# A network's first conditioning made feature tile by feature tile, with the first two hidden tiles multiplied behind each of them

## The chip, the cores and the metric

The kernel runs on one core of a Trainium2 chip. The metric is the device time of one execution in microseconds (us), lower is better. TensorE (PE in the profile, with its weight loads on a row of their own, PEld), VectorE (DVE), ScalarE (ACT) and GpSimd (POOL) work beside each other; the transfers that matter here are issued on SyncE's queue (SP), which takes them strictly in order.

## What is computed

The reference runs one transformer block and then two more blocks of another kind over 256 tokens of width 1024 (and a context of 256 tokens). Only the first lines of the first block touch the change:

```
mod = silu(c) @ w_ada + b_ada                 # (1, 9*1024)
sh1, sc1, gt1, ... = split(mod, 9)
y = rmsnorm(h, norm_ffn1) * (1 + sc1) + sh1   # 256 tokens x 1024 features
h = h + 0.5 * gt1 * swiglu(y, w_ffn1_gu, w_ffn1_down)
# swiglu: (silu(y @ w_gate) * (y @ w_up)) @ w_down, hidden width 2816 = 22 tiles of 128
```

The first conditioning is the pair sh1 and sc1: two vectors of 1024 values, each a product of silu(c) with a 1024 x 1024 piece of w_ada, 4 MB of f32 apiece. The first network cannot begin its matrix products before a feature tile of y (128 features x 256 tokens) has its scale and its shift.

## The kernel before

Activations lie feature-major: feature tile d of 8, 128 features on the partitions, tokens along the free dimension. Each f32 operand of a large product is split into a rounded high part and a remainder (H and L: `cut` and `split`, a cast on ACT, L149, and a subtraction on DVE, L150), and `mm3` (L172 to L174) issues three products H*H, H*L and L*H. For a hidden tile f of the network, `up` makes a gate and an up product, each over 8 feature tiles, 48 products of 256 columns in all; then silu, multiply and split give the hidden tile. 22 hidden tiles are followed by 8 output tiles (`down`) of 66 products each.

The start of the kernel (L664 to L706) does this, in program order:

1. Scale. The 4 MB of scale weights come in 8 loads `raw` (L672, 512 KB each, rows of a feature tile k). Each is the moving operand of products with the one column silu(c) as weights (L674), which gather the whole scale as two rows of 512 in two PSUM banks. f32 operands make every product two passes, so there are 32 passes of 512 columns. All 8 loads must be in before the scale is whole. The two rows are copied out and turned into columns by 8 products of one column (L689, 16 passes), and `settle` adds the bias and the gain.
2. The norm of x. Among the loads x arrives (1 MB, L676), and `row_of` broadcasts c over 128 partitions (L223). Squares on ACT, sums on DVE, `finish` (L329 to L343) leaves the reciprocal norm of each token, broadcast, in a PSUM bank.
3. u = x * scale * norm for 8 tiles (L693), then per tile the shift: `unit` loads 512 KB of transposed shift weights and sums their product with the broadcast silu(c) along the rows on DVE (L270). L701 (ACT) writes yH with the shift as bias, L702 (DVE) writes yL.
4. Three tiles of gate and up weights are loaded and cut in between (`ready`), and the context (1 MB, L704) is loaded behind the last shift tile; all later weight loads are queued behind that shift tile too (`first_loads`).

Hidden tiles f = 0 and f = 1 hold a bank each for gate and up (`mm`, `sc`, two buffers of each), so all four banks are open for them; from f = 2 on gate and up share one bank. Buffers: 8 slots for `raw`, 4 for the weight loads `wraw`, 3 each for their H and L.

The order of the instructions on each engine, and which load gets which slot, is fixed at build time by a planner that goes by program order as priority, by its own estimate of what is ready and by free slots. Later conditioning (`pump`) is put 400 places behind. Inside one PSUM bank the planner keeps writes of TensorE and reads of other engines in program order.

Of the kernel before, what the change touches and what calls it, by code (L numbers as in the profile page):

```python
# [10 lines left out]
F32 = mybir.dt.float32  # L11
BF16 = mybir.dt.bfloat16
F32R = mybir.dt.float32r
I32 = mybir.dt.int32
AF = mybir.ActivationFunctionType
OP = mybir.AluOpType
AX = mybir.AxisListType.X

P = 128
# [54 lines left out]
def trace(tc, A, dbg=None):  # L74
# [12 lines left out]
    def tl(pl, shape, dt, tag, bufs=None):  # L87
        kw = {} if bufs is None else {"bufs": bufs}
        return pl.tile(shape, dt, name=tag, tag=tag, **kw)

    def f32(ap):
        return ap.bitcast(F32)
# [11 lines left out]
    def bank(tag, shape=None):  # L104
        return tl(psum, shape or [P, 512], F32, tag)
# [70 lines left out]
    def split(H, L, x, copy=None):  # L176
        (copy or act.copy)(H, x)
        vec.tensor_tensor(L, x, f32(H), op=OP.subtract)  # L178
# [226 lines left out]
    def norm_of(seg, finish=True):  # L405
        n = Norm(seg)
        for d in range(ND):
            n.add(d)
        if finish:
            n.finish()  # L410
        return n


    def resid_add(ps, d, segs, keys, ch, norms):
        for s in segs:
# [4 lines left out]
            if norms is not None:  # L420
                norms[s].add(d)

    def up(w_gu, f, sub, hH, hL, tags):

        feed = Feed(w_gu, 2 * f)
        gH, gL = feed.next()
        uH, uL = feed.next()
        n = T * len(sub)
        ys = slice(sub[0] * T, sub[0] * T + n)
        if n == 512 or w_gu == "w1_gu" and f < 2:  # L430
            pg = bank("mm", [P, n])
            pu = bank("sc", [P, n])
        else:
            pb = bank(tags[f % 2])
            pg = pb[:, :T]
            pu = pb[:, T:]
        for ps, H, L in ((pg, gH, gL), (pu, uH, uL)):
            for k in range(ND):
                w = slice(k * P, k * P + P)
                mm3(ps, H[:, w], L[:, w], yH[:, k, ys], yL[:, k, ys], k == 0, k == ND - 1)  # L440
        sg = tl(tpool, [P, 512], F32, "sg", 2)
        act.activation(sg[:, :n], pg, AF.Silu)
        h = tl(tpool, [P, 512], F32, "hf", 2)
        vec.tensor_tensor(h[:, :n], sg[:, :n], pu, op=OP.mult)
        split(hH, hL, h[:, :n])

    def ahead(pools, w_gu, seg, out):

# [3 lines left out]
            up(w_gu, f, [seg], *out[f], ("mm", "mm"))  # L452
            yield

    def ffn_steps(hp, nslot, w_gu, w_dn, keys, gate_ch, segs, norms, lead=0, done=None, pre=None):

        N = T * len(segs)  # L460
        both = len(segs) == 2
        tags = ("mm", "sc")
        pre = pre or {}
        hs = {}

        def hidden(f):
            t = [tl(hp, [P, N], F32R, x, nslot) for x in ("hH", "hL")]
            hs[f] = {q: [x[:, i * T:i * T + T] for x in t] for i, q in enumerate(segs)}
            hs[f]["all"] = t
            if f in pre:  # L470
                hs[f][segs[1]] = pre[f]

        def ups(f, sub):
            up(w_gu, f, sub, *hs[f]["all" if len(sub) == len(segs) else sub[0]], tags)

        def down(ps, feed, k0, k1, part):
            whole = len(part) == len(segs) and not any(k in pre for k in range(k0, k1))
            W = [feed.block() for _ in range(k0, k1)]
            for i, q in enumerate(["all"] if whole else part):
                o = ps if whole else ps[:, i * T:i * T + T]  # L480
                for k in range(k0, k1):
                    mm3(o, *W[k - k0], *hs[k][q], k == k0, k == k1 - 1)

        groups = GROUPS if both or w_dn in GROUPED else ((0, NF),)
        for gi, (k0, k1) in enumerate(groups):
            last = gi == len(groups) - 1
            fs = list(range(k0, k1))
            if gi == 0 and lead:
                for f in fs[:lead]:
                    hidden(f)  # L490
                for i, q in enumerate(segs):
                    if i:
                        flush()
                    for f in fs[:lead]:
                        ups(f, [q])
                        tick(-(-ND // lead))
                        yield
                fs = fs[lead:]
            for f in fs:
                hidden(f)  # L500
                ups(f, segs[:1] if f in pre else segs)
                yield
            for q in segs:
                need(keys[q], gate_ch)
            for part in ([[q] for q in segs] if last else [segs]):
                feed = Feed(w_dn, k0)
                for d in range(ND):
                    ps = bank(tags[d % 2], [P, T * len(part)])
                    down(ps, feed, k0, k1, part)
                    resid_add(ps, d, part, keys, gate_ch, norms if last else None)  # L510
                    tick(1)
                    yield
                if last and done is not None:
                    flush()
                    for q in part:
                        done(q)

    def ffn(w_gu, w_dn, keys, gate_ch, segs, to, norms, done=None, lead=0, start=0.0, by=1.0, hook=None, pre=None,
            nslot=0):
        both = len(segs) == 2  # L520
        with ExitStack() as st:
            hp = pool("ffn_h", stack=st)
            steps = ffn_steps(hp, nslot or (12 if both or w_dn in GROUPED else 22), w_gu, w_dn, keys, gate_ch, segs, norms, lead, done, pre)
            n = NF + ND * (len(GROUPS) if both or w_dn in GROUPED else 1) + (lead + ND if both else 0)
            first = upos[0]
            for i in range(n):
                pump_to(first + (to - first) * min(1.0, max(0.0, (i + 1) / n - start) / (by - start)))
                next(steps)
                if hook is not None:
                    hook(i)  # L530
            for _ in steps:
                pass
# [129 lines left out]
    with ExitStack() as st:  # L662

        tp0 = pool("start", stack=st)  # L664
        csil = tl(tp0, [P, ND], F32, "csil")
        nc.sync.dma_start(csil, A["c_fm"])
        act.activation(csil, csil, AF.Silu)
        scp = [bank("sc", [1, 512]) for _ in range(2)]
        late = list(range(ND))
        for k in range(ND):  # L670
            raw = tl(tp0, [P, D], F32, "raw", 8)
            nc.sync.dma_start(raw, A["wada_sc"][k])  # L672
            for j in range(2):
                pe.matmul(scp[j], csil[:, k:k + 1], raw[:, j * 512:j * 512 + 512], start=k == 0, stop=k == ND - 1)  # L674
            if k == 1:
                nc.sync.dma_start(r[:, :, :T], A["xT"])  # L676
                row_of("c")
                nm = norm_of(0, False)
            if k == 4:
                nm.finish()  # L680
            if k in (3, 5):
                unit("wada", 0, late[0], s1, tl(tp0, [P, D], F32, "raw", 8))
                late.pop(0)
        pt = bank("tp", [P, ND])
        for j in range(2):
            row = tl(tpool, [P, 512], F32, "sg", 2)[:1, :]
            act.copy(row, scp[j])
            for d in range(4):
                pe.matmul(pt[:, 4 * j + d:4 * j + d + 1], row[:, d * P:d * P + P], one1, start=True, stop=True)  # L689
        settle("1", 1, pt)  # L690
        u = tl(tp0, [P, ND, T], F32, "u")
        for d in range(ND):
            vec.scalar_tensor_tensor(u[:, d, :], r[:, d, :T], modA["1"][:, d:d + 1], nm.rb, op0=OP.mult, op1=OP.mult)  # L693
        for d in range(ND):
            if d in late:
                dma = unit("wada", 0, d, s1, tl(tp0, [P, D], F32, "raw", 8))
                if d in (4, 5, 6):
                    ready["w1_gu", d - 4] = cut(load(A["w1_gu"][d - 4]))
            sh = mod["1"][:, d:d + 1]
            vec.tensor_tensor(sh, sh, V("b_ada", d), op=OP.add)  # L700
            act.activation(yH[:, d, :T], u[:, d, :], AF.Identity, bias=sh)  # L701
            vec.scalar_tensor_tensor(yL[:, d, :T], u[:, d, :], sh, f32(yH[:, d, :T]), op0=OP.add, op1=OP.subtract)  # L702
        first_loads[0] = dma
        queued(nc.sync.dma_start(r[:, :, T:], A["ctxT"]), dma)  # L704
        last_load[0] = dma
# [12 lines left out]
        if i >= NF - 1:  # L718
            run(nC[0], 1)

    ffn("w1_gu", "w1_dn", ["1"], 2, [0], upto["c0", 1], nm, next_norm(nm, ["1"], 1), hook=hook, by=FBY)
    run(fill, 2)
    tick(4)
    run(fill, 0)
# [720 lines left out]
def prepare(i):  # L1445
# [18 lines left out]
    for n in ("c", "c_2", "c_ctx_2"):  # L1464
        a[n] = i[n].reshape(-1)
    a["wada"] = _wt(i["w_ada"][0])
    a["wada_sc"] = i["w_ada"][0][:, D:2 * D].reshape(ND, P, D)
    a["c_fm"] = _fm(i["c"])
    a["wmod0"], a["wmod1"] = _wt(i["w_mod_2"][0]), _wt(i["w_mod_2"][1])
    for n, g, d in (("w1", "w_ffn1_gu", "w_ffn1_down"), ("w2", "w_ffn2_gu", "w_ffn2_down")):  # L1470
# [44 lines left out]
```

## Time and profile before

| | us |
|---|---|
| three runs, median (lowest to highest) | 2415.01 (2412.6 to 2419.7) |
| profiled execution, its own time | 2415.01 |
| span of the profiled execution, first to last instruction | 2413.3 |
| time outside the span | 1.7 |

The profile is of one execution. Times in it are from the start of the span. A matmul row on PE lasts longer than the distance to the next one, since products are pipelined: what a product costs in a stream is the distance between starts. The granted clock of TensorE has two levels here, 1.2 and 2.4 GHz (0.50 and 1.00 in the column PEclk); the column says 1.00 before the first recorded change, which lies at about 27 us.

### The profile page before, as it was taken

Reading aid. Unit: us, or ns where it says so; the run is one execution under the profiler, and the core shown is the slowest. Engines: PE = TensorE matmul, PEld = TensorE weight load, DVE = VectorE, ACT = ScalarE, POOL = GpSimd, SP = SyncE. Lnnn points to the kernel's source line nnn. Section 1 sums busy time; section 2 is a strip of 40 time slices with the busy share of each in tenths; the row PEclk is TensorE's granted clock in tenths of the full one; section 3 lists DMA queues with packets and bytes.
Section 4 is the critical chain, followed back from the end, with each engine's and each line's share of the span. In section 5 each row is a group of like instructions: output and inputs, shape, how many; then the busy total and the mean of one; then the engine's idle time right before and its main releaser. Section 6 shows DMA issues by size and latency. Waiting matters only on the chain.

```text
span 2413.3 us, 38351 instructions
## 1 busy us (share of the span) xinstructions
PE 2367.9 (98%) x15304; PEld 2127.8 (88%) x15304; DVE 1730.2 (72%) x3063; ACT 1029.8 (43%) x1549; POOL 47.4 (2%) x47
## 2 busy tenths in 40 slices
PE   7999999999999999998999999999999999999999
PEld 4999889999998888877988888998888988999999
DVE  6889987665998689789875556877454786565554
ACT  4444575444432236675632222542222563344442
POOL 0000000000000000230000000000000000000000
PEclk9999999999999999999999999999999999999999
DMA  8897865665674455411463434564444542244554
GB/s 317 318 311 249 310 219 170 207 214 207 226 243 170 151 192 195 157 62 55 158 218 131 157 140 149 175 210 175 175 175 165 186 154 96 97 135 147 193 186 145
DMA packets 124660, 442.75 MB, mean 183 GB/s; under 512 B 13984, under 2 KB 18208, under 8 KB 124352
## 3 DMA queue, kind: packets, MB, share of 16 engines
q1 hardware_dynamic: 123216, 436.30, 51.9%
q0 software_dynamic: 1120, 3.80, 0.5%
q8 instruction: 120, 1.97, 0.3%
q14 instruction: 60, 0.49, 0.1%
q10 hardware_dynamic: 144, 0.19, 0.0%
HBM read 439.19 MB, written 1.05 MB: 182 GB/s over the span
## 4 chain that ended last, share of the span: by engine, by line
PE 53%; DVE 2%; ACT 1%; issue 0%; ACTq 0%
PE mm L172 9%; PE mm L173 9%; PE mm L174 9%; PE sc L174 8%; PE sc L172 8%; PE sc L173 8%; PE tp L1227 1%; PE sm L172 1%; PE sm L173 1%; PE sm L174 1%; PE tp L574 1%; PE mm L1083 0%; ACT wH L149 0%; DVE wL L150 0%; PE sm L1008 0%
## 5 line engine op out<-in xcount | busy, mean ns | idle before, releaser
L149 ACT CAST wH<-wraw 128x1024 fp32r<-128x1024 f32 x598 | 626.3, 1049 | 1036.6 <-PE mm L173 374.6
L150 DVE TENSOR_TENSOR wL<-wraw,wH 128x1024 fp32r<-128x1024 f32 x586 | 716.2, 1224 | 346.5 <-ACT wH L149 336.5
L172 PE MATMUL mm<-yH,wH 128*128 128x256 f32 (+1 forms) x1736 | 553.4, 319 | 6.4 <-ACT wH L149 3.8
L174 PE MATMUL mm<-yH,wL 128*128 128x256 f32 (+1 forms) x1736 | 551.0, 317 | 3.5 <-DVE wL L150 3.5
L173 PE MATMUL mm<-yL,wH 128*128 128x256 f32 (+1 forms) x1736 | 551.5, 318 | 0.6 <-DVE yL L702 0.3
L174 PE MATMUL sc<-yH,wL 128*128 128x256 f32 (+1 forms) x1192 | 385.9, 324 | 5.7 <-DVE wL L150 5.5
L172 PE MATMUL sc<-yH,wH 128*128 128x256 f32 (+1 forms) x1192 | 387.0, 325 | 0.4 <-ACT wH L149 0.3
L173 PE MATMUL sc<-yL,wH 128*128 128x256 f32 (+1 forms) x1192 | 385.2, 323 | 0.0
L172 PEld LDWEIGHTS mm<-yH,wH 128*128 128x128 f32 x1736 | 328.7, 189 | 29.8 <-ACT wH L149 4.1
L174 PEld LDWEIGHTS mm<-yH,wL 128*128 128x128 f32 x1736 | 328.5, 189 | 26.7 <-DVE wL L150 4.2
L173 PEld LDWEIGHTS mm<-yL,wH 128*128 128x128 f32 x1736 | 328.5, 189 | 23.4 <-DVE yL L702 1.0
L270 DVE SCALAR_TENSOR_TENSOR mjunk<-mraw,crow_c 128x1024 bf16<-128x1024 f32 x200 | 244.2, 1221 | 26.6 <-DMA mraw<-in_wada_dram 15.2
L174 PEld LDWEIGHTS sc<-yH,wL 128*128 128x128 f32 x1192 | 225.5, 189 | 26.6 <-DVE wL L150 7.2
L172 PEld LDWEIGHTS sc<-yH,wH 128*128 128x128 f32 x1192 | 225.8, 189 | 20.8 <-ACT wH L149 1.0
L173 PEld LDWEIGHTS sc<-yL,wH 128*128 128x128 f32 x1192 | 225.6, 189 | 20.1 <-DVE yL L178 0.5
L174 PE MATMUL sc<-hH,wL 128*128 128x256 f32 (+1 forms) x636 | 191.9, 302 | 1.2 <-DVE wL L150 1.2
L172 PE MATMUL mm<-hH,wH 128*128 128x256 f32 (+1 forms) x636 | 192.9, 303 | 0.0
L173 PE MATMUL mm<-hL,wH 128*128 128x256 f32 (+1 forms) x636 | 192.4, 303 | 0.0
L172 PE MATMUL sc<-hH,wH 128*128 128x256 f32 (+1 forms) x636 | 192.2, 302 | 0.0
L174 PE MATMUL mm<-hH,wL 128*128 128x256 f32 (+1 forms) x636 | 191.9, 302 | 0.0
L173 PE MATMUL sc<-hL,wH 128*128 128x256 f32 (+1 forms) x636 | 191.8, 302 | 0.0
L270 DVE SCALAR_TENSOR_TENSOR mjunk<-mraw,crow_c_ctx 128x1024 bf16<-128x1024 f32 x112 | 137.0, 1223 | 4.5 <-ACT crow_c_ctx L224 2.5
(418 smaller groups left out, 3289.5 us busy)
## 6 DMA issues: line engine op xcount, KB each, us to landing
mraw<-in_wmod_dram SPq DMA_DIRECT2D x144, 512.0 KB, 4.6
wraw<-in_fa_gu_dram SPq DMA_DIRECT2D x116, 512.0 KB, 3.6
wraw<-in_fb_gu_dram SPq DMA_DIRECT2D x94, 512.0 KB, 3.3
wraw<-in_w_gu_dram SPq DMA_DIRECT2D x88, 512.0 KB, 4.0
wraw<-in_fa_dn_dram SPq DMA_DIRECT2D x60, 512.0 KB, 3.7
mraw<-in_wada_dram SPq DMA_DIRECT2D x56, 512.0 KB, 5.4
wraw<-in_fb_dn_dram SPq DMA_DIRECT2D x52, 512.0 KB, 3.3
wraw<-in_w_dn_dram SPq DMA_DIRECT2D x44, 512.0 KB, 3.4
```

The source lines that it names most:

```text
L149: act.copy(H, raw)
L150: (eng or vec).tensor_tensor(L, raw, f32(H), op=OP.subtract)
L172: pe.matmul(ps, aH, bH, start=start, stop=False)
L173: pe.matmul(ps, aH, bL, start=False, stop=False)
L174: pe.matmul(ps, aL, bH, start=False, stop=stop)
L270: queued(vec.scalar_tensor_tensor(junk, raw, 1.0, row_of(c), op0=OP.mult, op1=OP.mult, accum_out=mod[key][:, ch * 8 + j:ch * 8 + j + 1]), ...
L574: pe.transpose(pt[:, j * P:j * P + P], src(j), ident)
L1227: pe.matmul(ps[:, c], kT[:, j, jt * P:jt * P + P], qT[:, j, :], start=j == 0, stop=j == 1)
```

## The change

The scale weights are laid out anew by the host, so that load d holds all that feature tile d of the scale needs. Behind the norm, which now comes first, one loop over the 8 feature tiles makes the scale of tile d (8 products with the weight block as stationary operand and the one column silu(c) moving, 16 passes of one column), its shift, its u, yH and yL, and behind them the products of hidden tiles 0 and 1 that need feature tile d, in four banks opened for the purpose (hidden tile 1 begins at d = 3, with its first four feature tiles at once). The four weight tiles for them are split into buffers of their own. `raw` has 4 slots in place of 8. The network then takes hidden tiles 0 and 1 as begun and only applies silu, multiply and split (`gate`).

```diff
+    def gate(pg, pu, n, hH, hL):
+        sg = tl(tpool, [P, 512], F32, "sg", 2)
+        act.activation(sg[:, :n], pg, AF.Silu)
+        h = tl(tpool, [P, 512], F32, "hf", 2)
+        vec.tensor_tensor(h[:, :n], sg[:, :n], pu, op=OP.mult)
+        split(hH, hL, h[:, :n])
...
-        if n == 512 or w_gu == "w1_gu" and f < 2:
+        if n == 512:
...
             for f in fs:
                 hidden(f)
-                ups(f, segs[:1] if f in pre else segs)
+                if begun is not None and 2 * f < len(begun):
+                    gate(begun[2 * f], begun[2 * f + 1], T, *hs[f]["all"])
+                else:
+                    ups(f, segs[:1] if f in pre else segs)
                 yield
...
-        scp = [bank("sc", [1, 512]) for _ in range(2)]
-        late = list(range(ND))
-        for k in range(ND):
-            raw = tl(tp0, [P, D], F32, "raw", 8)
-            nc.sync.dma_start(raw, A["wada_sc"][k])
-            for j in range(2):
-                pe.matmul(scp[j], csil[:, k:k + 1], raw[:, j * 512:j * 512 + 512], start=k == 0, stop=k == ND - 1)
-            if k == 1:
-                nc.sync.dma_start(r[:, :, :T], A["xT"])
-                row_of("c")
-                nm = norm_of(0, False)
-            if k == 4:
-                nm.finish()
-            if k in (3, 5):
-                unit("wada", 0, late[0], s1, tl(tp0, [P, D], F32, "raw", 8))
-                late.pop(0)
+        sc1 = tl(tp0, [P, ND], F32, "sc1")
+        vec.tensor_scalar(sc1, V("b_ada", 8, 8), 1.0, None, op0=OP.add)
+        nc.sync.dma_start(r[:, :, :T], A["xT"])
+        row_of("c")
+        nm = norm_of(0)
         pt = bank("tp", [P, ND])
...
-        settle("1", 1, pt)
-        u = tl(tp0, [P, ND, T], F32, "u")
+        begun = [bank(t, [P, T]) for t in ("mm", "sc", "mm", "sc")]
+        parts = []
+        done = [0, 0]
         for d in range(ND):
-            vec.scalar_tensor_tensor(u[:, d, :], r[:, d, :T], modA["1"][:, d:d + 1], nm.rb, op0=OP.mult, op1=OP.mult)
...
+            raw = tl(tp0, [P, D], F32, "raw", 4)
+            nc.sync.dma_start(raw, A["wada_sc"][d])
+            for k in range(ND):
+                pe.matmul(pt[:, d:d + 1], raw[:, k * P:k * P + P], csil[:, k:k + 1], start=k == 0, stop=k == ND - 1)
+            a = modA["1"][:, d:d + 1]
+            vec.scalar_tensor_tensor(a, pt[:, d:d + 1], sc1[:, d:d + 1], V("norm_ffn1", d), op0=OP.add, op1=OP.mult)
+            dma = unit("wada", 0, d, s1, tl(tp0, [P, D], F32, "raw", 4))
             sh = mod["1"][:, d:d + 1]
             vec.tensor_tensor(sh, sh, V("b_ada", d), op=OP.add)
...
+            u = tl(tpool, [P, T], F32, "hn", 3)
+            vec.scalar_tensor_tensor(u, r[:, d, :T], a, nm.rb, op0=OP.mult, op1=OP.mult)
+            act.activation(yH[:, d, :T], u, AF.Identity, bias=sh)
+            vec.scalar_tensor_tensor(yL[:, d, :T], u, sh, f32(yH[:, d, :T]), op0=OP.add, op1=OP.subtract)
+            if d in (0, 2):
+                for i in range(d, d + 2):
+                    x = load(A["w1_gu"][i])
+                    H, L = [tl(tp0, [P, D], F32R, f"first{n}{i}") for n in "HL"]
+                    split(H, L, x)
+                    parts.append((H, L))
+            for t in range(len(parts) // 2):
+                while done[t] <= d and (t == 0 or d >= 3):
+                    k = done[t]
+                    w = slice(k * P, k * P + P)
+                    for i in (2 * t, 2 * t + 1):
+                        H, L = parts[i]
+                        mm3(begun[i], H[:, w], L[:, w], yH[:, k, :T], yL[:, k, :T], k == 0, k == ND - 1)
+                    done[t] += 1
...
-    a["wada_sc"] = i["w_ada"][0][:, D:2 * D].reshape(ND, P, D)
+    a["wada_sc"] = i["w_ada"][0][:, D:2 * D].reshape(ND, P, ND, P).transpose(2, 1, 0, 3).reshape(ND, P, D)
```

## Rows read from the trace of the kernel before

**Rows 1.** The page: the span, and TensorE's busy time (share) and instructions.
```profile
span 2413.3 us, 38351 instructions
...
PE 2367.9 (98%) x15304; PEld 2127.8 (88%) x15304; DVE 1730.2 (72%) x3063; ACT 1029.8 (43%) x1549; POOL 47.4 (2%) x47
```

**Rows 2.** Stretches: length, then busy us (instructions) by engine, clock, DMA share, GB/s.
```profile
core 0: us, PE busy (x) PEld busy (x) DVE busy (x) ACT busy (x) POOL busy (x), PEclk, DMA share, GB/s
2.00:8.00 6.00, 3.08 (x4) 0.50 (x5) 0.00 (x0) 0.72 (x2) 0.00 (x0) 1.00 0.90 300
8.00:26.00 18.00, 16.23 (x49) 4.54 (x48) 7.29 (x19) 6.20 (x13) 0.00 (x0) 1.00 1.03 407
26.00:34.00 8.00, 2.20 (x12) 1.52 (x11) 6.89 (x17) 3.19 (x5) 0.00 (x0) 0.58 1.03 396
34.00:38.00 4.00, 3.70 (x17) 3.40 (x17) 4.00 (x10) 1.95 (x3) 0.00 (x0) 0.56 1.01 370
38.00:50.00 12.00, 10.66 (x81) 9.79 (x80) 10.60 (x22) 8.75 (x17) 0.00 (x0) 1.00 0.54 183
50.00:140.00 90.00, 90.00 (x759) 90.00 (x759) 75.88 (x114) 41.41 (x62) 0.00 (x0) 1.00 0.88 320
...
180.00:220.00 40.00, 40.00 (x336) 40.00 (x335) 39.73 (x62) 16.66 (x19) 0.00 (x0) 1.00 0.80 281
```

**Rows 3.** SyncE's queue in order of time: start, length, line, transfer, count.
```profile
2.22 0.65 SPq L676 DMA_DIRECT2D resid<-in_xT_dram  x1
...
10.38 1.58 SPq L672 DMA_DIRECT2D raw<-in_wada_sc_dram  x2
...
24.39 0.55 SPq L704 DMA_DIRECT2D resid<-in_ctxT_dram  x1
```

**Rows 4.** TensorE's products in order of time; in brackets the idle time before, its releaser.
```profile
4.92 6.20 PE L674 MATMUL sc<-raw,csil 128*1 128x512 f32 x8 [4.92 <-DMA raw<-in_wada_sc_dram]
...
25.09 1.94 PE L689 MATMUL tp<-one,sg 1*128 1x1 f32 x16
...
34.22 0.58 PE L174 MATMUL mm<-yH,wL 128*128 128x256 f32 x1 [2.49 <-DVE wL L150]
34.60 0.41 PE L172 MATMUL mm<-yH,wH 128*128 128x256 f32 x1
...
36.94 0.41 PE L172 MATMUL mm<-yH,wH 128*128 128x256 f32 x1
...
50.04 0.28 PE L172 MATMUL mm<-yH,wH 128*128 128x256 f32 x1
```

**Rows 5.** Weight loads of f32 products with few columns, in order of time.
```profile
16.42 0.30 PEld L329 LDWEIGHTS tp<-ones,sqacc 128*128 128x128 f32 x2 [0.86 <-issue]
...
17.09 0.30 PEld L330 LDWEIGHTS tp<-ones,sq 128*128 128x128 f32 x2
...
2216.29 0.93 PEld L343 LDWEIGHTS sm<-ident,nm_rs 128*128 128x128 f32 x4 [1.75 <-issue]
```

**Rows 6.** Line 343 alone: shortest, median, longest ns of one instruction.
```profile
L343 PEld LDWEIGHTS sm<-ident,nm_rs x52: 185/189/337, 19.2 to 2216.9; 128*128 128x128 f32 x52
```

**Rows 7.** DVE by line in the first 50 us: busy us, mean ns, idle before.
```profile
L270 DVE SCALAR_TENSOR_TENSOR mjunk<-raw,crow_c 128x1024 bf16<-128x1024 f32 x8 | 9.8, 1222 | 4.3 <-DMA raw<-in_wada_dram 4.3
L150 DVE TENSOR_TENSOR wL<-wraw,wH 128x1024 fp32r<-128x1024 f32 x5 | 6.1, 1222 | 0.8 <-ACT wH L149 0.8
L321 DVE TENSOR_TENSOR sqacc<-sqacc,sq 128x256 f32<-128x256 f32 x12 | 5.1, 425 | 11.0 <-ACT sq L319 10.1
...
L693 DVE SCALAR_TENSOR_TENSOR u<-resid,moda,sm 128x256 f32<-128x256 f32 x8 | 3.2, 477 | 0.0
L700 DVE TENSOR_TENSOR mod<-mod,vecs 128x1 f32<-128x1 f32 x8 | 1.2, 156 | 0.1
```

**Rows 8.** The tile yH before 80 us: ns shortest/median/longest, first and last start.
```profile
L701 ACT ACTIVATE yH<-u,mod x8: 492/508/511, 28.0 to 43.0; 128x256 fp32r<-128x256 f32 x8
L702 DVE SCALAR_TENSOR_TENSOR yL<-u,mod,yH x8: 479/480/485, 30.6 to 43.7; 128x256 fp32r<-128x256 f32 x8
```

More of the change, by code (lines that the diff above doesn't have):

```diff
@@ L440, in up @@
                 mm3(ps, H[:, w], L[:, w], yH[:, k, ys], yL[:, k, ys], k == 0, k == ND - 1)
[L441 to L445, printed above, removed]
+        gate(pg, pu, n, hH, hL)
     def ahead(pools, w_gu, seg, out):
@@ L453, in ahead, with ffn_steps @@
             yield
-    def ffn_steps(hp, nslot, w_gu, w_dn, keys, gate_ch, segs, norms, lead=0, done=None, pre=None):
+    def ffn_steps(hp, nslot, w_gu, w_dn, keys, gate_ch, segs, norms, lead=0, done=None, pre=None, begun=None):
         N = T * len(segs)
@@ L518, in ffn @@
     def ffn(w_gu, w_dn, keys, gate_ch, segs, to, norms, done=None, lead=0, start=0.0, by=1.0, hook=None, pre=None,
-            nslot=0):
+            nslot=0, begun=None):
         both = len(segs) == 2
@@ L522, in ffn @@
             hp = pool("ffn_h", stack=st)
-            steps = ffn_steps(hp, nslot or (12 if both or w_dn in GROUPED else 22), w_gu, w_dn, keys, gate_ch, segs, norms, lead, done, pre)
+            steps = ffn_steps(hp, nslot or (12 if both or w_dn in GROUPED else 22), w_gu, w_dn, keys, gate_ch, segs, norms, lead, done, pre, begun)
             n = NF + ND * (len(GROUPS) if both or w_dn in GROUPED else 1) + (lead + ND if both else 0)
@@ L684, in trace @@
-        pt = bank("tp", [P, ND])
[L685 to L689, printed above, removed]
-        settle("1", 1, pt)
-        u = tl(tp0, [P, ND, T], F32, "u")
-        for d in range(ND):
-            vec.scalar_tensor_tensor(u[:, d, :], r[:, d, :T], modA["1"][:, d:d + 1], nm.rb, op0=OP.mult, op1=OP.mult)
@@ L694, in trace @@
[L694 to L698, printed above, removed]
+        sc1 = tl(tp0, [P, ND], F32, "sc1")
[3 more added lines that the diff above has]
+        nm = norm_of(0)
+        pt = bank("tp", [P, ND])
+        begun = [bank(t, [P, T]) for t in ("mm", "sc", "mm", "sc")]
@@ L699, in trace @@
             sh = mod["1"][:, d:d + 1]
             vec.tensor_tensor(sh, sh, V("b_ada", d), op=OP.add)
-            act.activation(yH[:, d, :T], u[:, d, :], AF.Identity, bias=sh)
-            vec.scalar_tensor_tensor(yL[:, d, :T], u[:, d, :], sh, f32(yH[:, d, :T]), op0=OP.add, op1=OP.subtract)
+            u = tl(tpool, [P, T], F32, "hn", 3)
+            vec.scalar_tensor_tensor(u, r[:, d, :T], a, nm.rb, op0=OP.mult, op1=OP.mult)
+            act.activation(yH[:, d, :T], u, AF.Identity, bias=sh)
@@ L719, in hook @@
             run(nC[0], 1)
-    ffn("w1_gu", "w1_dn", ["1"], 2, [0], upto["c0", 1], nm, next_norm(nm, ["1"], 1), hook=hook, by=FBY)
+    ffn("w1_gu", "w1_dn", ["1"], 2, [0], upto["c0", 1], nm, next_norm(nm, ["1"], 1), hook=hook, by=FBY,
+        begun=begun)
     run(fill, 2)
```

## The prediction

> **What bounds the kernel now.** I read the page first: TensorE is marked busy for 98% of the span [rows 1]. A busy TensorE is only a sign that something was in its pipe, so I cut the start into stretches [rows 2]. Four things are to be seen there. From 8 to 26 us the transfers run at their ceiling, 407 GB/s with a share of 1.03. From 26 to 34 TensorE has 2.20 us of work in 8 and the clock falls to the half level (0.58 on average). From 34 to 50 it gets going: half clock until about 37, and DVE occupied for 4.00 of 4 and then 10.60 of 12 us. From 50 to 140 it never waits: 759 products in 90.00 us, 0.1186 us each, with DVE at 84% and the transfers at 0.88. So what is at stake lies before 50 us. After it TensorE alone sets the pace, and I take it that whatever moves the first product of hidden tile 2 moves the end by as much. That product starts at 50.04 [rows 4], and 50.0 is the number to compare with.
>
> The yardsticks for TensorE: in a stream a 256-column product costs 0.1186 us at 2.4 GHz, as above, and at 1.2 GHz (36.94 - 34.60) / 11 = 0.213, with ten products between the two rows [rows 4]. A one-column pass is set by its weight load: the six passes from 16.42 to 17.09 give 0.112 at the higher clock. At the lower one no such stream is shown; the nearest is four loads in 0.93, of which the last takes 0.337 (the longest of that line), so (0.93 - 0.337) / 3 = 0.198 [rows 5, 6].
>
> **The change, part by part.** *Removed:* 32 wide scale passes, 16 passes that turn the rows, two row copies and the settling. All lie before 27.03, in time in which TensorE waited for loads anyway; taking them out gains nothing by itself. But they are also what held the clock up: the last passes before the fall are one-column ones, from 25.09 to 27.03 [rows 4], and the clock's mean of 0.58 over 26 to 34 puts the fall soon behind them.
>
> *Added on TensorE:* 8 scale tiles of 16 one-column passes, 16 x 0.112 = 1.79 us each at full clock and 16 x 0.198 = 3.17 at half. The 96 products of hidden tiles 0 and 1 stay: 11.4 us at full clock, 20.4 at half. At full clock, the scale therefore costs more than the products it sits between, and unlike before it shares the path with them.
>
> *Moved: the order of transfers.* x and c go first; so far x is issued at 2.22 behind two scale loads, the last two scale loads from 10.38, and the context, after all of the conditioning, at 24.39 [rows 3]. Behind them come, per tile, scale and shift load of 0.524 MB each, and two pairs of weight loads. TensorE's stretch begins with scale tile 2: norm, scale 0 and 1 are done while loads arrive. By 8 us 6 x 300 = 1.8 MB have moved; up to scale load 2 there are 1.05 + 0.52 + 7 x 0.524 = 5.24 MB, or 6.29 if weight tiles 2 and 3, which have slots at once, slip ahead. At 407 GB/s that is 16.5 or 19.0 us; I take 17.7.
>
> *From there, the sum for TensorE.* It starts at half clock, as the kernel begins so: 8 wide passes in 6.20, 0.78 each [rows 4]. Scale tiles 2 and 3: 2 x 3.17 = 6.3. Hidden tile 0 with feature tiles 0 to 2: 18 x 0.213 = 3.8. At d = 3 there are 30 products in a row, and I let the clock come back as it did behind 34.22, where products at the half-clock distance run until about 37 and the stretch from 38 has 1.00 [rows 2, 4]: 14 x 0.213 = 3.0. That is 30.8 us. The rest at full clock: 64 x 0.1186 = 7.6 and four scale tiles 4 x 1.79 = 7.2, so 45.6 if it never waits.
>
> *Waits.* Between scale d and its products stand the small DVE scale step, u, yH and yL: 0.156 + 0.477 + 0.508 + 0.480 = 1.62 us [rows 7, 8]. The next scale tile (1.79) can hide this, but only if its load is in and the reader of the shared PSUM bank is past; with 4 `raw` slots load d + 2 isn't asked for before scale d is done or shift d summed. So each of the last five tiles loses between 0 and 1.62, 0 to 8.1 together. I take 5: DVE is loaded almost as heavily as TensorE, so most links will queue behind a 1.22 us sum or split.
>
> *Behind the last product.* Hidden tiles 0 and 1 now end together, so hidden tile 2 can't have its bank before silu of tile 0 is through: 0 to 0.5 us (an ACT pass of this size, 0.508 [rows 8]); I take 0.5. The weights of hidden tile 2 stand on SP behind the last shift load and the context, but at 51 us they have long landed. Hidden tile 2 starts at 45.6 + 5 + 0.5 = 51.1, 1.1 later than before.
>
> *DVE and ACT.* Nothing is added that isn't removed elsewhere; the u and the sums merely start earlier. DVE's total up to the last yL is 8 x (1.22 + 0.48 + 0.48 + 0.16 + 0.16) = 20.0, four splits 4.9 and six sums 2.6 [rows 7, 8], 27.5 us from about 6 on, so 33 at the earliest. It is not the bound unless TensorE is quick; before, its last yL came at 43.7 + 0.5 [rows 8].
>
> *The price of a weight load at half clock* is the softest term. The Trainium skill ("TensorE: Matmul & The Clock Gate", section LDWEIGHTS) has a load's time go by its columns alone, 128 of them in 107 ns, and doesn't tell the two clocks apart. By that an estimate for a scale tile would be 1.7 us at either clock and the sum would be 2.9 lower. The row shows 0.198, on four loads only, and I keep the row.
>
> **The rivals.**
>
> *A. TensorE comes up to full clock early and the loop streams (faster).* The place is the first three tiles. Then from 16.5 or 19.0 there remain 6 x 1.79 + 11.4 = 22.1, an end of 38.6 to 41.1. The other limits allow that: the last shift load, (12.05 - 1.8) / 0.407 + 8 = 33.2, then its sum, bias, yH, yL and 12 products, 3.8 more, 37.0; and hidden tile 2's first weights 3.9 us of transfers and a split behind it, about 38.3. That is 9 to 11.4 us gained: 2403.6 to 2406. For it: wide products are sprinkled in from tile 0 on. Against: the passes ahead are one-column ones, and the clock fell behind such passes at 27 us. It decides if the clock column shows 1.00 from about 20 us on.
>
> *B. The clock stays at half through the loop (slower).* The scale tiles cut the wide products into bursts of 6 or 12, 1.3 to 2.6 us long, and each burst waits for its own feature tile. If the burst at d = 3 is broken up too, the sum is 17.7 + 6 x 3.17 + 20.4 = 57.1, and 0 to 5 of waits: 7 to 12 later, 2422 to 2427. It decides from a half-clock stretch of more than some 14 us beyond my 13. For it: the fall at 27. Against: the rise within 3 us of 34.22, although products there still had gaps. The Trainium skill (same page, section HAM oscillation) warns against just this form, a little product work per k-tile between waits for loads, where every tile starts at the low clock; it advises taking all k-tiles together, as the kernel before nearly does. The trace bears out the fall and the rise, not yet the oscillation.
>
> *C. The shift is swallowed.* From 180 to 220 DVE is occupied for 39.73 of 40 us [rows 2]. If conditioning work, not TensorE, sets the end of that stage, or if the planner's new order loses or gains elsewhere as much, a difference of some us at 50 doesn't arrive: 2415, no change. Against: TensorE has no gap in that stretch either.
>
> **How the numbers follow.** The profiled execution took 2415.01 in its own time, equal to the median of the runs; the span of 2413.3 plus 1.7. Adding 1.1 gives 2416. A difference under 0.3%, 7.2 us, can't be told from no change here. The likeliest case, with waits of 0 to 8.6, reaches from 2410.6 to 2419.7, chance 0.60, nearly all of it inside that band. A has 0.12, B 0.20, C 0.08. Faster 0.12 (A), same 0.66 (the likeliest but 0.02 of it, and C), slower 0.22 (B and that 0.02). The range from 2406 to 2426 holds the likeliest, C, A's upper edge and most of B; outside are A's floor and B's last us.
>
> **What will show it.** Right, if in the new profile scale passes of one column stand in groups of 16 between bursts of products; the clock is low until 27 to 33 us and full after; the first product of hidden tile 2 starts between 46 and 55 us; 50 us later TensorE streams at 0.119 as before. A shows as that product at 38 to 43; B as low clock until 45 or later and the product beyond 55. The weights of hidden tile 2 arriving after the last product of tile 1 would show that I was wrong to hide them. A time off by more than the shift of that product would show that the rest of the order changed, which I don't forecast.

## The result and the profile after

The changed kernel took 2438.32 us (median of 4 runs, 2436.31 to 2440.91) beside 2417.27 for the kernel before (4 runs, 2412.6 to 2419.7): a ratio of 1.0092, 95% interval 1.008 to 1.0105. It is slower, by about 21 us, and 12 us above the upper end of the forecast range.

The page of the profile after, its span and its busy times [rows 1]:

```profile
span 2434.6 us, 38519 instructions
...
PE 2386.2 (98%) x15384; PEld 2161.0 (89%) x15384; DVE 1732.1 (71%) x3070; ACT 1029.5 (42%) x1547; POOL 47.4 (2%) x47
```

TensorE is occupied 18 us longer at nearly the same number of instructions. The stretches of the profile after, columns as in [rows 2]:

```profile
20.00:36.00 16.00, 14.27 (x58) 12.89 (x59) 9.52 (x17) 4.01 (x6) 0.00 (x0) 1.00 0.67 228
36.00:54.80 18.80, 18.80 (x93) 18.80 (x92) 6.61 (x17) 1.52 (x3) 0.00 (x0) 1.00 0.45 147
54.80:61.60 6.80, 6.27 (x50) 5.65 (x49) 4.45 (x11) 0.51 (x1) 0.00 (x0) 0.97 0.92 331
61.60:71.40 9.80, 7.27 (x30) 6.68 (x31) 6.31 (x11) 7.84 (x15) 0.00 (x0) 0.50 0.55 206
71.40:161.40 90.00, 90.00 (x761) 90.00 (x760) 76.00 (x115) 42.85 (x64) 0.00 (x0) 1.00 0.90 329
```

From 36 to 54.8 TensorE never waits, DVE is occupied for 6.61 of 18.8 us and the transfers run at 0.45: TensorE alone is the bound there. The clock column doesn't help, since it reads 1.00 before the first recorded change, which lies near 61.2 here. The distances tell the clock. TensorE in order of time, in the profile after, the rows that answer to [rows 4]:

```profile
25.90 3.58 PE L687 MATMUL tp<-csil,raw 128*128 128x1 f32 x16
...
32.45 0.58 PE L172 MATMUL mm<-yH,firstH 128*128 128x256 f32 x1 [1.05 <-ACT yH L695]
...
36.10 3.41 PE L687 MATMUL tp<-csil,raw 128*128 128x1 f32 x16
39.37 0.56 PE L172 MATMUL mm<-yH,firstH 128*128 128x256 f32 x1
39.73 0.41 PE L173 MATMUL mm<-yL,firstH 128*128 128x256 f32 x1
39.94 0.42 PE L174 MATMUL mm<-yH,firstL 128*128 128x256 f32 x1
...
41.65 3.41 PE L687 MATMUL tp<-csil,raw 128*128 128x1 f32 x16
...
47.62 3.41 PE L687 MATMUL tp<-csil,raw 128*128 128x1 f32 x16
...
53.61 2.21 PE L687 MATMUL tp<-csil,raw 128*128 128x1 f32 x16
...
57.57 1.84 PE L687 MATMUL tp<-csil,raw 128*128 128x1 f32 x16
...
66.60 0.58 PE L172 MATMUL mm<-yH,wH 128*128 128x256 f32 x1 [1.28 <-ACT wH L149]
```

L687 is a scale tile. From 41.65 to 47.62 one round of the loop takes 5.97 us, 16 passes and 12 products. Products stand 0.21 apart (39.73 to 39.94), the passes of a tile (39.37 - 36.10) / 16 = 0.204: both are at 1.2 GHz. A scale tile falls from 3.41 to 2.21 and 1.84 only at 53.61 and 57.57; by its 2.21 the clock rises at about 54.4. From 61.2 to 71.4 it is half clock again (0.50 in the column). The first product of hidden tile 2 starts at 66.60 where it was 50.04 [rows 4], 16.6 us later. Behind it the distance still grows. Hidden tile 2 runs at half clock until 71.4, and the next norm's broadcast starts 17.8 us later (192.76 against 174.99). At the one behind it the distance is 20.3 (259.21 against 238.95), for the clock is down once more, in a stretch in which the kernel before reads 1.00:

```profile
252.40:259.10 6.70, 6.43 (x30) 6.43 (x31) 4.12 (x10) 1.00 (x4) 1.11 (x2) 0.50 0.97 333
```

24 products stand in it, 0.094 us longer each (0.213 against 0.119), some 2.3 us by this estimate. Why the clock fell there isn't shown. Then the distance stays between 19.7 and 20.9.

DVE in the first 66.6 us of the profile after: line, busy us, mean ns, idle time ahead.

```profile
L270 DVE SCALAR_TENSOR_TENSOR mjunk<-raw,crow_c 128x1024 bf16<-128x1024 f32 x8 | 9.7, 1218 | 0.0
...
L689 DVE SCALAR_TENSOR_TENSOR moda<-tp,sc,vecs 128x1 f32<-128x1 f32 x8 | 1.7, 218 | 25.1 <-PE tp L687 25.1
```

DVE's sums cost what they cost before [rows 7], but for 25.1 us it stands idle waiting for scale passes.

### The profile page after: what moved, and what is told of

Read it like the earlier page. It is cut to its first block, busy times and chain, and to the rows that moved or that the text cites. A ratio compares the mean times of both kernels' runs of the same rounds, so it can differ in the third digit from the quotient of the medians.

```text
span 2434.6 us, 38519 instructions
## 1 busy us (share of the span) xinstructions
PE 2386.2 (98%) x15384; PEld 2161.0 (89%) x15384; DVE 1732.1 (71%) x3070; ACT 1029.5 (42%) x1547; POOL 47.4 (2%) x47
## 4 chain that ended last, share of the span: by engine, by line
PE 53%; DVE 2%; ACT 1%; issue 0%; ACTq 0%
PE mm L172 9%; PE mm L173 8%; PE mm L174 8%; PE sc L172 8%; PE sc L174 8%; PE sc L173 8%; PE sm L172 1%; PE sm L173 1%; PE sm L174 1%; PE tp L1236 1%; PE tp L580 1%; PE mm L1092 0%; ACT wH L149 0%; PE sm L1017 0%; DVE wL L150 0%
## 5 line engine op out<-in xcount | busy, mean ns | idle before, releaser
L174 PE MATMUL sc<-yH,wL 128*128 128x256 f32 (+1 forms) x1176 | 380.7, 324 | 3.6 <-DVE wL L150 3.6
```

The lines of the kernel that those rows point to most:

```text
L174: pe.matmul(ps, aL, bH, start=False, stop=stop)
```

## The experiments

**Theory 1.** The 128 one-column scale passes now stand on the path of TensorE, and with them the loop stays at half clock. **Theory 2 (rival).** The passes are bearable; what costs is where the products stand, the late weights of hidden tile 2, the new order of loads or the 4 slots.

Each time stands beside runs of the kernel before on the same chip; "hidden tile 2" is the start of its first product in the profiled execution.

**The two halves of the change, one at a time.** `e1_scale_before` keeps the old scale and its 8 slots and puts only the products behind the feature tiles; `e2_scale_tiles` makes the scale by tiles and leaves the products where they were.

The core of e1 against the changed kernel (the wide passes, their turning and settling stand ahead of the loop again), then of e2:

```diff
-            for k in range(ND):
-                pe.matmul(pt[:, d:d + 1], raw[:, k * P:k * P + P], csil[:, k:k + 1], start=k == 0, stop=k == ND - 1)
...
+            for j in range(2):
+                pe.matmul(scp[j], csil[:, k:k + 1], raw[:, j * 512:j * 512 + 512], start=k == 0, stop=k == ND - 1)
```
```diff
-                        mm3(begun[i], H[:, w], L[:, w], yH[:, k, :T], yL[:, k, :T], k == 0, k == ND - 1)
...
+            if d < 3:
+                ready["w1_gu", d] = cut(load(A["w1_gu"][d]))
```

> One half of the change alone: the scale is made as before (eight loads, wide passes, rows turned into columns), and only the products of hidden tiles 0 and 1 are written behind each feature tile, with their four weight tiles in buffers of their own. Theory 1, the 128 one-column scale passes and the half clock that goes with them are the loss: the first product of hidden tile 2 comes back to 46 to 52 us (50.0 before, 66.6 after) and the time to within 6 us of the kernel before, 2410 to 2423. Theory 2, the loss is the products' new place behind each feature tile, their waits and the late weights of hidden tile 2: that product stays beyond 60 us and the time at 2430 or more.

> The other half alone: the scale feature tile by feature tile with one-column passes, norm first, four slots; hidden tiles 0 and 1 are left to the network's own code as before, with three weight tiles loaded early. Theory 1 (scale passes and half clock): no better than the whole change, first product of hidden tile 2 at 60 us or later, 2430 to 2445. Theory 2 (products behind each feature tile): back to within 6 us of the kernel before, 2410 to 2423.

e1: 2414.49, ratio 0.9984 (0.9971 to 0.9998), hidden tile 2 at 49.15. e2: 2438.46, ratio 1.0091 (1.0073 to 1.011), scale tiles of 3.41 to 3.55 throughout. The whole loss is in the scale by tiles; the products' new place costs nothing and may gain some 4 us. In e1 the clock is back at 34.9, and a round takes 2.0 us, set by DVE (occupied for 21.73 of 22 us from 28 to 50). TensorE in the profile of e1:

```profile
34.72 0.34 PE L173 MATMUL mm<-yL,firstH 128*128 128x256 f32 x1
34.90 0.28 PE L174 MATMUL mm<-yH,firstL 128*128 128x256 f32 x1
...
40.30 0.39 PE L173 MATMUL mm<-yL,firstH 128*128 128x256 f32 x1 [0.26 <-DVE yL L709]
42.31 0.38 PE L173 MATMUL mm<-yL,firstH 128*128 128x256 f32 x1 [0.26 <-DVE yL L709]
```

**Idle wide work on TensorE.** `e3_dense_ahead` adds 15 wide f32 products (30 passes) into a spare bank ahead of the loop, `e4_dense_tiles` also 4 (8 passes) in each tile. Their result is used by nothing. The last added line is e4's alone:

```diff
+        def dense(m):
+            ps = bank("sm", [P, T])
+            for q in range(m):
+                pe.matmul(ps, ident, vecs[:, :T], start=True, stop=True)
...
+        dense(15)
         nm = norm_of(0)
...
+            dense(4)
             a = modA["1"][:, d:d + 1]
```

> The changed kernel with 15 f32 products of 256 columns (30 passes) into a spare bank put ahead of everything on TensorE, where it is idle until 11.4 us; their result is not used. If only the start at half clock is at fault and the loop can hold the clock once it is up: full clock from about 8 us on, scale tiles of 1.8 us, the first product of hidden tile 2 near 50 us, 2415 to 2424. If the one-column passes and the waits let the clock fall, and the loop can't bring it back: half clock again before 25 us, more than half of the loss stays, 2428 to 2440.

> The same with four more such products (8 passes, 1.7 us at full and 3.4 at half clock) in each of the eight tiles: 14 to 27 us of useless work on the path. If the clock is what costs, and lack of wide work is why it is low: full clock through the loop, 20 + 7 x 1.8 + 11.4 + 13.7 + some 4 of waits, first product of hidden tile 2 near 62 us, 2427 to 2434, no slower than the changed kernel although it does more. If the clock stays at half, or if it never was the cost: the work adds 14 to 27 us, 2450 or more.

e3: 2434.08, ratio 1.0072 (1.0051 to 1.0094), hidden tile 2 at 62.12. e4: 2432.55, ratio 1.0069 (1.005 to 1.0088), at 61.35: more work for TensorE in every tile, and yet no slower than the changed kernel (the intervals touch, so neither is shown to be faster). Scale tiles in the profile of e3, then of e4:

```profile
12.41 1.93 PE L693 MATMUL tp<-csil,raw 128*128 128x1 f32 x16
16.63 3.33 PE L693 MATMUL tp<-csil,raw 128*128 128x1 f32 x16 [2.29 <-DVE moda L695]
...
36.52 2.27 PE L693 MATMUL tp<-csil,raw 128*128 128x1 f32 x16
...
41.24 3.41 PE L693 MATMUL tp<-csil,raw 128*128 128x1 f32 x16
```
```profile
28.64 1.84 PE L693 MATMUL tp<-csil,raw 128*128 128x1 f32 x16
...
43.76 1.84 PE L693 MATMUL tp<-csil,raw 128*128 128x1 f32 x16
```

In e3 the clock is full at first, gone one scale tile and a wait of 2.29 later, back in the scale tile at 36.52, behind 21 products, and gone again just before the one at 41.24. In e4 it stays from 28.64 on. So the half clock is a cost of its own.

**The slots.** `e5_slots8`:

```diff
-            raw = tl(tp0, [P, D], F32, "raw", 4)
+            raw = tl(tp0, [P, D], F32, "raw", 8)
...
```

> The changed kernel with 8 slots for the scale and shift loads in place of 4, so that the load of scale tile d + 2 no longer waits for scale tile d to be done; nothing else differs. If the scale passes and their half clock set the pace (theory 1), the loads come earlier but TensorE has the same 20 us of scale tiles and 18 us of products: at most the 6.4 us of waits can go, hidden tile 2's first product at 60 to 66 and the time at 2432 to 2439. If the ring of 4 slots sets the pace (rival), loads run at the transfer ceiling from the start, the scale tiles queue up densely, and that product comes at 50 to 55: 2422 to 2427.

2434.31, ratio 1.0074 (1.0052 to 1.0096). Loads come early, and scale tile 2 starts at 25.74 (25.90 in the changed kernel). In the profiled execution TensorE is occupied from 36 to 66 for 29.81 of 30 us, rounds of 16 passes and 12 products, all at half clock by their distances; hidden tile 2 at 70.02.

```profile
36.00:66.00 30.00, 29.81 (x140) 29.51 (x140) 11.44 (x30) 2.78 (x6) 0.00 (x0) 1.00 0.39 141
```

The ring of slots isn't the cause, and in this execution a loop without gaps didn't bring the clock back. That execution took 2440.81; the other three were 4.7 to 8.5 us shorter and left no profile.

**No scale passes, and half of them.** `e6_scale_dve` sums the scale on DVE like the shift; `e7_half_passes` leaves out every second scale product.

```diff
-                pe.matmul(pt[:, d:d + 1], raw[:, k * P:k * P + P], csil[:, k:k + 1], start=k == 0, stop=k == ND - 1)
+            unit("wada", 1, d, s1, tl(tp0, [P, D], F32, "raw", 4), plain=True)
```
```diff
-            for k in range(ND):
+            for k in range(0, ND, 2):
...
```

> The changed kernel with each tile's scale summed by DVE as the shift is, so that TensorE has no scale passes; order, slots and products behind each tile stay. DVE gets 8 more sums of 1.22 us (9.8 us). Theory 1 (the 128 passes and the half clock): TensorE's loop holds only 96 products, DVE becomes the bound at about 37 us of work from 14 on, hidden tile 2's first product at 51 to 58 and the time at 2416 to 2425. If the cause is the products' place, the late weights of hidden tile 2 or the order of the loads, that product stays beyond 62 and the time above 2432.

> The changed kernel with every second scale product left out (8 passes per tile in place of 16; half of the scale's sum is missing), all loads as before. Theory 1 with 0.204 us a pass: 56 to 64 passes on the path are gone, 11 to 13 us, hidden tile 2's first product at 53 to 56 and the time at 2424 to 2428; if the clock also comes back earlier, down to 2420. If waits for loads or for the small DVE steps set the pace, the passes only give way to waits: under 4 us gained, 2434 or more.

e6: 2421.95, ratio 1.0017 (1.0008 to 1.0027), hidden tile 2 at 51.70. e7: 2424.19, ratio 1.003 (1.0018 to 1.0041), at 54.05. Both as theory 1 has it; but in e7 the clock is also back at about 39.8 (the scale tile at 39.41, of 8 passes, takes 1.16 after 1.70), 14.6 us before the changed kernel, so fewer passes and the clock aren't parted there. The profile of e6, TensorE in order of time and the stretch of its loop:

```profile
28.67 0.32 PE L174 MATMUL mm<-yH,firstL 128*128 128x256 f32 x1
28.82 0.28 PE L173 MATMUL sc<-yL,firstH 128*128 128x256 f32 x1
...
32.52 0.39 PE L172 MATMUL mm<-yH,firstH 128*128 128x256 f32 x1 [2.11 <-ACT yH L691]
...
47.83 0.39 PE L172 MATMUL mm<-yH,firstH 128*128 128x256 f32 x1 [3.27 <-ACT yH L691]
...
51.70 0.58 PE L172 MATMUL mm<-yH,wH 128*128 128x256 f32 x1 [1.97 <-ACT sg L425]
```
```profile
28.70:49.20 20.50, 10.86 (x73) 9.02 (x73) 17.99 (x44) 4.09 (x10) 0.00 (x0) 1.00 0.88 302
...
49.40:51.70 2.30, 0.33 (x3) 0.04 (x2) 1.25 (x2) 2.27 (x4) 0.00 (x0) 0.50 0.46 183
```

Here the clock comes back at 28.7, in the long group of products at d = 3, just where I had forecast it for the changed kernel. It holds for 20.5 us, though TensorE is occupied for only 10.86 of them, and waits of 1.1 to 2.1 do it no harm. Behind the wait of 3.27 it goes, at 49.2, with no scale pass near, and hidden tile 2 starts at half clock, until 56. DVE, with 8 more sums, is the bound (17.99 of 20.50).

**The same passes, wide.** `e8_row_passes` swaps the operands: silu(c) is the stationary column, the 128 x 128 block moves.

```diff
-                pe.matmul(pt[:, d:d + 1], raw[:, k * P:k * P + P], csil[:, k:k + 1], start=k == 0, stop=k == ND - 1)
+            ps = bank("sm", [1, P])
+            for k in range(ND):
+                pe.matmul(ps, csil[:, k:k + 1], raw[:, k * P:k * P + P], start=k == 0, stop=k == ND - 1)
+            row = tl(tpool, [P, 512], F32, "sg", 2)[:1, :P]
+            act.copy(row, ps)
+            pe.matmul(pt[:, d:d + 1], row, one1, start=True, stop=True)
```

> The changed kernel with the operands of the scale products swapped: the silu column is the stationary side (one column), the 128x128 block moves, so the 128 passes are 128 columns wide; each tile's row is copied by ACT and turned by 2 one-column passes. If the one-column form is what keeps the clock low, full clock comes with the burst at d = 3 and stays: scale tiles of some 2 us or less from there, hidden tile 2's first product at 50 to 58 with 0.7 us per tile for copy and turn, 2422 to 2429. If it is the number of passes and the waits between short bursts, whatever their form, it stays at half clock and the copies come on top: 66 to 72 and 2438 to 2444.

2422.86, ratio 1.0025 (1.0012 to 1.0037), hidden tile 2 at 58.61 although each tile has a copy and two turning passes more. Scale passes and one product in the profile of e8, and a stretch of its loop:

```profile
20.41 3.57 PE L688 MATMUL sm<-raw,csil 128*1 128x128 f32 x16
...
24.17 0.28 PE L172 MATMUL sc<-yH,firstH 128*128 128x256 f32 x1
...
33.37 2.33 PE L688 MATMUL sm<-raw,csil 128*1 128x128 f32 x16
...
42.01 1.69 PE L688 MATMUL sm<-raw,csil 128*1 128x128 f32 x14
```
```profile
31.00:34.00 3.00, 3.00 (x14) 2.39 (x15) 3.00 (x5) 0.66 (x1) 0.00 (x0) 0.50 0.39 139
```

A pass costs about the same as in one-column form, but the clock is up at 24, right behind two scale tiles, where the changed kernel has it at 54.4. It is gone once, from 30.8 to 34.1, and then full to the end of the loop.

**The same passes beside the path.** `e10_passes_beside` is e6 with 16 one-column passes a tile in TensorE's gaps, used by nothing.

```diff
+            ps = bank("tp", [P, ND])
+            for k in range(ND):
+                pe.matmul(ps[:, :1], f32(yL[:, d, :P]), vecs[:, k:k + 1], start=k == 0, stop=k == ND - 1)
...
```

> The version with the scale summed by DVE (loop bound by DVE at 3.3 us a tile, TensorE occupied for half of it and at full clock from 28.7 on, hidden tile 2's first product at 51.7), with 16 one-column passes per tile put into TensorE's gaps; their result goes into a spare bank and is used by nothing. At full clock they need 1.8 of the 1.9 us free in each tile. If one-column passes pull the clock down by themselves, the products fall back to 0.213 and a tile takes 2.6 + 3.3 = 5.9 us: that product at 62 to 68 and 2432 to 2440. If it was the waits and the order that kept the clock low, the passes hide in the gaps at 0.112: 52 to 56 and 2421 to 2426.

2423.43, ratio 1.0034 (1.002 to 1.0049), hidden tile 2 at 53.75. TensorE in the profile of e10:

```profile
31.41 3.41 PE L674 MATMUL tp<-vecs,yL 128*128 128x1 f32 x16
...
37.60 0.31 PE L174 MATMUL sc<-yH,firstL 128*128 128x256 f32 x1
...
38.21 1.84 PE L674 MATMUL tp<-vecs,yL 128*128 128x1 f32 x16
...
41.41 1.84 PE L674 MATMUL tp<-vecs,yL 128*128 128x1 f32 x16
```

This falls against the strong form of theory 1, that one-column passes pull the clock down by themselves: with as many of them as the changed kernel the clock comes back at 37.6 and stays, a round takes 41.41 - 38.21 = 3.20 us. It does come back 9 us later than without them (e6). And it gives the price of the clock: a round of the same passes and products, 3.20 at full, 5.97 at half.

**One long group of products.** In the changed kernel the 30 products of d = 3 don't stand in a row: by the trace 8 stand ahead of scale tile 3 (36.10; 6 of d = 2 are before them), 10 behind it, and the last 12 behind scale tile 4 (41.65). `e11_pairs` takes two feature tiles at a time, `e12_one_burst` starts the second hidden tile's loads one tile later. As written it also loads weight blocks 3 and 4 in place of 2 and 3, so hidden tile 1 is computed with other weights of the same size.

```diff
+            for e in (d, d + 1) if d % 2 == 0 else ():
+                raw = tl(tp0, [P, D], F32, "raw", 4)
+                nc.sync.dma_start(raw, A["wada_sc"][e])
...
-            for t in range(len(parts) // 2):
+            for t in range(len(parts) // 2 if d % 2 else 0):
```
```diff
-            if d in (0, 2):
+            if d in (0, 3):
```

> The changed kernel with the feature tiles taken two at a time: the scale passes of both, then shift, norm step and products of both. In the built order one group of 24 products stands unbroken between scale tiles where the changed kernel has 14 and 10 on either side of one. If the length of an unbroken group of products is what brings the clock back, it is full from there and a scale tile falls from 3.41 to 1.84: hidden tile 2's first product at 54 to 60, 2424 to 2430. If the one-column passes keep the clock low whatever the grouping: 63 to 69 and 2434 to 2441.

> The changed kernel with the weights of hidden tiles 2 and 3 of this stage's second pair loaded behind feature tile 3 in place of 2; in the built order the second pair then catches up in one group of 36 products, as the prediction had assumed for the changed kernel (30), where it really has 20, a scale tile and 10. If one long group brings the clock back, full clock comes some 3 us into it and the four scale tiles behind run at 1.84: first product of the next hidden tile at 55 to 60, 2425 to 2430. If not, half clock lasts as in the changed kernel: 65 to 69, 2436 to 2441.

e11: 2441.69, ratio 1.0105 (1.0088 to 1.0122), hidden tile 2 at 72.53. e12: 2436.36, ratio 1.0082 (1.0067 to 1.0097), at 69.12. TensorE in the profile of e12:

```profile
43.27 0.39 PE L174 MATMUL sc<-yH,firstL 128*128 128x256 f32 x1
43.49 0.29 PE L172 MATMUL sc<-yH,firstH 128*128 128x256 f32 x1
...
44.21 1.84 PE L687 MATMUL tp<-csil,raw 128*128 128x1 f32 x16
46.36 3.10 PE L687 MATMUL tp<-csil,raw 128*128 128x1 f32 x16 [0.31 <-DVE moda L689]
...
52.55 3.41 PE L687 MATMUL tp<-csil,raw 128*128 128x1 f32 x16
```

The long group does bring full clock, 5.7 us into it, but two scale tiles in a row follow, since the next products wait for their yH and yL, and the clock is gone in the second. In e11 likewise it is up at 42.9 and gone by 46.8. Both of my expectations were half wrong: grouping lifts the clock and doesn't keep it.

**A try at a faster kernel.** `e9_before_pool` is e1 with the four low halves subtracted on GpSimd.

```diff
-                    split(H, L, x)
+                    act.copy(H, x)
+                    nc.gpsimd.tensor_tensor(L, x, f32(H), op=OP.subtract)
```

> The version with the scale as in the kernel before (32 wide passes) and the products of hidden tiles 0 and 1 behind each feature tile (DVE full from 28 to 50, hidden tile 2's first product at 49.15), with the four subtractions of the weights' low halves moved from DVE to GpSimd. If DVE's 4 x 1.22 = 4.9 us stand on its path, that product comes at 44 to 46 and the time at 2409 to 2412, a ratio of 0.996 to 0.998. If the loads, ACT or TensorE end last there, or GpSimd's subtraction lands later than the products want it: 49 or beyond and a ratio of 0.998 to 1.001.

2423.80, ratio 1.0032 (1.0021 to 1.0042), a miss. GpSimd needs 2.33 to 3.38 us for a subtraction that takes DVE 1.22; its last one starts at 36.46, and the weights of hidden tile 2 come late (51.74, behind a wait of 2.31 for its wH).

## Why the prediction was wrong

**Two terms of the sum failed: where TensorE's stretch begins, and where the clock comes back.** From my 51.1 for hidden tile 2 to the measured 66.6 there are 15.5 us.

**The larger, 8.2 us, is "TensorE's stretch begins with scale tile 2: norm, scale 0 and 1 are done while loads arrive".** I took 17.7; scale tile 2 starts at 25.90. No load holds it: in e5 its load comes early and it starts at 25.74. I had overlooked that the scale passes stand in the norm's way. The norm's passes are over at about 13.3, but scale tile 0 follows them (13.17, at half clock), and on DVE the rest of the norm stands behind the small scale step that waits for that tile. DVE in the profile of the changed kernel:

```profile
16.76 0.22 DVE L689 SCALAR_TENSOR_TENSOR moda<-tp,sc,vecs 128x1 f32<-128x1 f32 x1 [5.37 <-PE tp L687]
16.90 0.15 DVE L334 TENSOR_SCALAR nm_xh<-tp 128x2 f32<-128x2 f32 x1
```

So the first product comes at 20.23 (17.89 in e6, without scale passes), and scale tile 1 behind the first products (22.19).

**The second, 5.9 us, is "at d = 3 there are 30 products in a row, and I let the clock come back as it did behind 34.22".** My half-clock part was 13.1 us long. In the changed kernel half clock lasts to about 54.4, and comes again from 61.2 to 71.4. From scale tile 2 on, six scale tiles take 16.9 us where I had 13.5, and 90 products 16.9 where I had 14.4 for 96. The last 1.4 us are waits (5.5 where I had 5) and the step behind the last product (1.5 where I had 0.5). Either term alone would have left that product at 59.3 or 57.0, by my own rule 2424 or 2422 and inside the range.

What the half clock costs in all is another question. From the first product at 20.23 to the end of the last at 65.1 there are 44.9 us: 112 scale passes, 80 of them at 0.204 and two tiles in 2.07 and 1.70, 20.1; 72 products at 0.213, 15.3; 24 at 0.1186, 2.9; 6.6 are left for waits and switches. At full clock the same work would be 112 x 0.106 + 96 x 0.1186 = 23.3, so the half clock costs 15.0. By that, an estimate from these rows, hidden tile 2 would have started at 51.6, and still no gain. That this lies near my 51.1 is luck: mine had 13.1 us of half clock in it and began 8.2 earlier.

Point by point:

- *What bounds it.* Right in the main: the shift at hidden tile 2 (16.6) is most of what arrives at the end (21). "By as much" was wrong: 4.7 us more come behind it in the profiled executions, 2.5 of them in the stretch where the clock is down from 252.4 to 259.1. Rival C, a shift that is swallowed, did not come.
- *The price of a pass.* Right: 0.204 at half clock (I had 0.198) and 0.106 at full (0.112). By an estimate from the Trainium skill ("TensorE: Matmul & The Clock Gate", section LDWEIGHTS) a scale tile would be 1.7 at either clock; the runs show 3.27 and 1.70, and the measurement decides. (With 1.7 for all six tiles my sum would have been 3.2 lower, not 2.9.)
- *The burst at d = 3.* Wrong twice. It was assumed from the program's order, but the planner broke it up (8, a scale tile, 10, a scale tile, 12). And e12 shows that even unbroken it gives full clock only from 43.4 to 46.9, as one-column passes and waits follow. What I had compared it with, the start behind 34.22 in the kernel before [rows 4], had products alone behind it. I had noted that the fall at 27 came behind one-column passes, and didn't carry that into the loop.
- *The removed passes lie "in time in which TensorE waited for loads anyway".* Misread: from 8 to 26 TensorE is occupied for 16.23 of 18 us [rows 2]. No term of the sum hangs on it.
- *Waits of 5.* Right in size: 5.5. (The range 2410.6 to 2419.7 counts the 0.5 behind the last product once too often at its upper end.)
- *The weights of hidden tile 2 are hidden.* Wrong, small: they are issued at 54.23, and the first products wait 1.28 and 0.46.
- *DVE not the bound.* Right for the changed kernel; it is in e1 and e6.
- *Rival B* was the right mechanism with its burst "broken up too", but came short: it started from 17.7 and gave 57.1 to 62.1; with the start at 25.90 it would have been 65.3 to 70.3, around the 66.6. The Trainium skill had warned of a form like it, short work between waits (same page, section HAM oscillation). The trace agrees in part: e3 falls behind a wait of 2.29 and e6 behind one of 3.27, but e5 stays at half through 30 us in which TensorE hardly waits (29.81 of 30), and the changed kernel falls at 61.2 out of a stretch with 6.27 of 6.8 us occupied.
- *Rival A* did not come: from 20 to 36 the distances are those of half clock.

**What stays open.** What lifts and holds the clock in a loop of both kinds of passes. e5 and e10 have rounds of the same 16 passes and 12 products, without gaps; one stays at half for 30 us, the other, once at full, stays there. The changed kernel and e5 give TensorE the same work up to 53.6, and only in the first does the clock rise, at 54.4: one profile of a version doesn't settle it. No run moves the late start alone. And e10's runs fall into two groups, seven from 2419.3 to 2424.3 and three from 2432.3 to 2433.7; only one of the first was profiled, so that the three lack the clock is argued, not shown.

## What to carry to other kernels

Before work is moved between products on TensorE, ask in what form it comes: many short one-column passes cost as much as the products they part (a scale tile 3.27, 12 products 2.56 us at half clock), and here the loop with them on its path ran at half clock to 54.4, where every product beside them cost nearly double. Ask too what else waits in order behind the first of them: here it was the norm, and that was the larger miss. A clock that came back in one stretch of a trace is evidence only for what stands behind it there; check in the built order, not in the source, whether the same group of products exists. If a matrix-vector product has to stand in such a loop, the matrix as the moving side (e8) or another engine (e6) is cheaper; leaving it ahead of the loop (e1) was cheaper still.

## What was not expected of the hardware

- One-column f32 passes double their time with the clock like wide ones: 0.106 and 0.204 us a pass, although each moves a single column. The forecast had this from four loads alone.
- With the operands swapped (one column to load, 128 moving) a pass costs hardly more than with 128 to load and one moving (3.57 against 3.41 to 3.58 a tile at half clock, 1.69 for 14 against 1.84 for 16 at full), but the clock was up at 24 with it and at 54.4 without.
- A wait took the clock with no scale pass near, but not at once: in e6 it fell at 49.2, 1.4 us behind the wait of 3.27, with the products between still 0.12 apart. In the changed kernel it fell at 61.2 with hardly a wait before.
